# Gate products of two heads in one PSUM tile, the last sums by token tile, and a warm-up of ten products

## The chip, the cores and the metric

The kernel runs on one core of one Trainium2 chip. The time is device microseconds of one execution, from three runs: a median of 764.66 us (764.39 to 766.47). The core has five engines that work side by side: TensorE (PE, with its weight loads shown as PEld), VectorE (DVE), ScalarE (ACT), GpSimd (POOL) and SyncE (SP), which here only issues DMAs. Each engine runs its own list of instructions in order; a semaphore lets one wait for another.

## What is computed

One layer of a decoder block, for 512 tokens of 1024 channels, all float32:

```python
p = x @ W_in + b_in      # u | v | q | k | v | r | low-rank gate | branch gates g_A, g_B
y_A = gelu(u) * (W_s @ layer_norm(gelu(v)) + b_s)      # in chunks of 128 tokens
log_f = log_sigmoid(a_low @ w_gate2 + b_gate) / 16     # the gate of linear attention
y_B = norm(gla(q, k, v, log_f)) * silu(r)              # 4 heads, key width 128, value width 256
m = sigmoid(g_A) * y_A + sigmoid(g_B) * y_B
h = layer_norm(2**0.25 * x + m @ W_out)
out = layer_norm(2**0.25 * h + relu(h @ W_1)**2 @ W_2)  # hidden width 4096
```

## The kernel before

**Products.** Every float32 operand is split into a high and a low part (`split`, L91 to L93: ScalarE writes the high part, VectorE the difference), and a product of two operands takes three passes on TensorE. The weights come in chunks of 128 x 1024, read by SyncE's queue into three raw buffers (`raw`, L114), split into `wh` and `wl`, of which there are seven pairs. A raw buffer is free for the next read once both halves of the split are done.

**Stages.** The start (L240 to L267) warms TensorE with products of ones (`wu`, L241) while the first input arrives, and then makes q and k of the first two heads (`first`). The values v of the gating unit follow in two halves of four token tiles each (`row_unit`, `ps` L208). Then come eight groups of u, q and k of the last two heads, the values, the branch gates and W_out, and last the feed-forward part, three quarters of which use a seven-product scheme (`m`, L898) for two-by-two blocks of quarters, and the last quarter plain products (`f`, L984).

**Attention beside it.** A plan by slots (`plan_pair`) puts the work of linear attention between these groups: after each group of 24 matmuls on TensorE, one slot's jobs are issued. For a pair of heads that is: the gate products (`gates`, L358) and from them `lf` and its running sum `cum`; for three levels the differences `kt` on VectorE (L403) and `qt` on GpSimd (L413), their exponentials on ScalarE (L424, L425), the products with k and q on VectorE (L426, L431), and the scores on TensorE (`sc`, L472), which VectorE copies under a mask into `AT` (L484).

**Values of the gating unit.** Each token tile of v passes VectorE (`vt`, L579), ScalarE's gelu (L581), VectorE's statistics (L582) and, in the second half, an aggregate (L564), three small instructions on GpSimd (`rs_sg`, L171, L174, L566) and the normalisation on ScalarE (L567).

**Order.** TensorE's instructions stand as the code writes them. Up to the end of W_out the order on VectorE, ScalarE and GpSimd is chosen by a scheduler from the dependences and its own estimates; behind that point it is the code's. So a change in one place can move instructions of other engines a long way off. ScalarE loads a table (`ACT_TABLE_LOAD`) whenever the next function is not in the one it holds.

**PSUM.** There are eight banks of 512 columns: four for `ps_m` (main products), two for `ps_a` (one tile of 512 columns in each, tag `aux`) and two for `ps_s` (one tile of 1024 columns, tag `sc`, for scores). The two gate products of a pair go to two `aux` tiles, which they share with `pa`, `pm`, `pt`, `po` and `pb`.

**Last stage.** The quarters of the feed-forward output lie in `acc`. `together` (L905) adds up whole quarters of two token tiles (128 x 1024 elements) and folds in the residual; most of it runs between the last of the seven products and the first plain products, and inside the first token tile of these.

## Time and profile before

| | |
|---|---|
| median of three runs | 764.66 us (764.39 to 766.47) |
| the profiled execution | 764.65 us, its span 762.9 us |
| TensorE busy | 750.0 us (98%) |
| VectorE busy | 489.4 us (64%) |
| ScalarE busy | 356.3 us (47%) |
| GpSimd busy | 68.1 us (9%) |
| mean granted TensorE clock | 0.996 |

Times of the profile are counted from the first instruction of the span. The profiled execution lies 1.7 us above its span and within 0.01 us of the median, so that what moves the span can be added to either. A row of the timeline gives start, duration, engine, line, operation, what is written from what, the count, and in brackets the idle time before it and what ended that. Instructions overlap a little: a matmul of 512 columns lasts 0.39 us by its row, and the next begins 0.23 us after it.

### The profile page before, as it was taken

The page shows a single profiled execution, that of the slowest core. Times are in us where ns is not written, and L with a number is a line of the kernel's source. Part 1 is how long each engine was busy: PE and PEld are TensorE (multiplying, and loading weights), DVE is VectorE, ACT ScalarE, POOL GpSimd, SP SyncE. Part 2 cuts the span into 40 slices and gives each one's busy share as a digit, 9 for nine tenths or more (in the row PEclk, how much of TensorE's full clock was granted, in tenths as well). Part 3 has the DMA queues.
Part 4 walks back from the last instruction along what each step waited for, and adds up shares of the span by engine and source line. Part 5 has one row for each costly group of instructions (what it writes and reads, how often), then busy time and mean ns, then how long its engine had stood idle before and what let it go on. Part 6 is the DMA issues. An engine that isn't in the chain of part 4 may idle for free.

```text
span 762.9 us, 8863 instructions
## 1 busy us (share of the span) xinstructions
PE 750.0 (98%) x3504; PEld 628.3 (82%) x3504; DVE 489.4 (64%) x587; ACT 356.3 (47%) x457; POOL 68.1 (9%) x86
## 2 busy tenths in 40 slices
PE   9998999999999999999999999999999999999996
PEld 8887888878888888888888988888888888888785
DVE  7369767668766542454548535774678667778975
ACT  7376864354146444444322444554554544445300
POOL 1015400013302212000001000000000000000011
PEclk9999999999999999999999999999999999999999
DMA  8523332110341232323231423444244433434111
GB/s 338 201 97 104 104 131 82 61 53 26 111 138 56 78 129 82 113 90 104 89 125 63 153 83 99 136 148 142 73 148 139 138 109 113 164 112 165 56 56 55
DMA packets 25465, 85.15 MB, mean 112 GB/s; under 512 B 3088, under 2 KB 3344, under 8 KB 25424
## 3 DMA queue, kind: packets, MB, share of 16 engines
q1 hardware_dynamic: 25280, 84.33, 32.7%
q8 instruction: 27, 0.44, 0.2%
q10 hardware_dynamic: 144, 0.26, 0.1%
q14 instruction: 14, 0.11, 0.0%
HBM read 82.48 MB, written 2.10 MB: 111 GB/s over the span
## 4 chain that ended last, share of the span: by engine, by line
PE 88%; DVE 5%; ACT 3%; issue 2%; POOL 1%; DVEq 0%; POOLq 0%
PE f L602 23%; PE m L898 14%; PE ps L208 12%; PE gb L602 6%; PE r L602 6%; PE u L602 6%; PE f L984 5%; PE ga L602 4%; PE first L265 3%; PE qk L602 2%; PE sc L472 2%; DVE wl L93 1%; POOL qt L413 1%; PE po L498 1%; PE po L500 1%
## 5 line engine op out<-in xcount | busy, mean ns | idle before, releaser
L93 DVE TENSOR_TENSOR wl<-raw,wh 128x1024 fp32r<-128x1024 f32 x141 | 175.0, 1251 | 137.2 <-ACT wh L92 130.6
L92 ACT CAST wh<-raw 128x1024 fp32r<-128x1024 f32 x141 | 145.3, 1045 | 122.7 <-PE ps L208 27.5
L602 PE MATMUL f<-xh,wh 128*128 128x512 f32 (+1 forms) x288 | 105.4, 366 | 0.0
L602 PE MATMUL f<-xl,wh 128*128 128x512 f32 (+1 forms) x288 | 105.2, 365 | 0.0
L602 PE MATMUL f<-xh,wl 128*128 128x512 f32 (+1 forms) x288 | 105.2, 365 | 0.0
L898 PE MATMUL m<-wh,oh 128*128 128x512 f32 x168 | 65.4, 389 | 0.0
L898 PE MATMUL m<-wl,oh 128*128 128x512 f32 x168 | 65.4, 389 | 0.0
L898 PE MATMUL m<-wh,ol 128*128 128x512 f32 x168 | 65.4, 389 | 0.0
L602 PEld LDWEIGHTS f<-xh,wl 128*128 128x128 f32 x288 | 54.3, 189 | 8.8
L602 PEld LDWEIGHTS f<-xl,wh 128*128 128x128 f32 x288 | 54.3, 189 | 8.7
L602 PEld LDWEIGHTS f<-xh,wh 128*128 128x128 f32 x288 | 54.3, 189 | 8.6
L208 PE MATMUL ps<-wh,xh 128*128 128x512 f32 x128 | 51.3, 401 | 0.0
L208 PE MATMUL ps<-wl,xh 128*128 128x512 f32 x128 | 50.1, 391 | 0.0
L208 PE MATMUL ps<-wh,xl 128*128 128x512 f32 x128 | 50.1, 391 | 0.0
L827 ACT ACTIVATE F<-f 128x512 f32<-128x512 f32 (+1 forms) x28 | 15.0, 537 | 72.4 <-PE f L602 72.4
L127 DVE TENSOR_TENSOR raw<-raw,raw 128x1024 f32<-128x1024 f32 x30 | 36.7, 1222 | 8.4 <-DMA raw<-in_w_all 8.4
L413 POOL TENSOR_TENSOR qt<-cum 128x768 f32<-128x768 f32 (+2 forms) x18 | 31.4, 1774 | 115.8 <-DVE cum L368 102.9
L898 PEld LDWEIGHTS m<-wl,oh 128*128 128x128 f32 x168 | 31.6, 188 | 6.6
L898 PEld LDWEIGHTS m<-wh,ol 128*128 128x128 f32 x168 | 31.5, 188 | 6.6
L898 PEld LDWEIGHTS m<-wh,oh 128*128 128x128 f32 x168 | 31.5, 188 | 6.5
L993 POOL TENSOR_TENSOR rs_l<-rs_l,nhalf 128x1 f32<-128x1 f32 x4 | 4.0, 988 | 328.6 <-DVE rs_l L992 328.6
L92 ACT CAST oh<-d 128x1024 fp32r<-128x1024 f32 x15 | 15.8, 1050 | 36.4 <-DVE d L824 36.4
(231 smaller groups left out, 1528.5 us busy)
## 6 DMA issues: line engine op xcount, KB each, us to landing
raw<-in_w_all SPq DMA_DIRECT2D x136, 512.0 KB, 3.3
bufB<-in_head SPq DMA_DIRECT2D x4, 512.0 KB, 7.9
xr<-in_x SPq DMA_DIRECT2D x8, 256.0 KB, 3.7
out<-bufA SPq DMA_DIRECT2D x8, 256.0 KB, 2.0
bufA<-in_head SPq DMA_DIRECT2D x3, 512.0 KB, 5.3
brow<-in_b_in SPq DMA_DIRECT2D x4, 256.0 KB, 5.9
g<-in_ln_g SPq DMA_DIRECT2D x2, 512.0 KB, 4.4
b<-in_ln_b SPq DMA_DIRECT2D x2, 512.0 KB, 4.3
```

What stands on the lines that cost most here:

```text
L92: nc.scalar.copy(hi, src)
L93: nc.vector.tensor_tensor(lo, src, hi.bitcast(F32), op=ALU.subtract)
L127: nc.vector.tensor_tensor(raw, raw, other[0], op=ALU.add if STREAM[i][0] == "sum" else ALU.subtract)
L208: nc.tensor.matmul(ps, s_, m_, start=(k == 0 and i == 0), stop=(k == KT - 1 and i == 2))
L265: nc.tensor.matmul(first[e], s_, m_[:, k, :], start=(k == 0 and i == 0), stop=(k == KT - 1 and i == 2))
L413: getattr(nc, DIFF_Q).tensor_tensor(qv[:, :, s0 : s0 + n, :], c4[:, :, d:4, :], c4[:, :, 0:n, h - 1 : h].broadcast_to([P, na, n, h]), op=A ...
L472: nc.tensor.matmul(sc[:, c, 0:192], pr.kt[:, jc * P : (jc + 1) * P], pr.qt[:, jc, :], start=True, stop=True)
L498: nc.tensor.matmul(po, pr.AT[:, j, c, :], vs, start=True, stop=(c == 0))
L602: nc.tensor.matmul(ps, s_, m_, start=(k == 0 and i == 0), stop=(k == KT - 1 and i == 2))
L827: nc.scalar.activation(dst, ps, AF.Relu)
L898: nc.tensor.matmul(ps, s_, m_, start=(k == 0 and i == 0), stop=(k == 3 and i == 2))
L984: nc.tensor.matmul(ps, s_, m_, start=(f == 0 and i == 0), stop=(f == 7 and i == 2))
```

## The change

- The warm-up is ten products of 128 columns instead of seven of 128 and five of 64. Each product of ones shows as two records.
- The two gate products of a pair go into the two halves of one `ps_s` tile, tag `sc`, instead of two `aux` tiles.
- `together` works on one token tile (128 x 512) at a time. Before the last stage only the sums for token tile 0 of quarter 7 remain; the others are written into the last stage, behind the statistics of a piece.

```diff
-WARM = (128,) * 7 + (64,) * 5
+WARM = 10
-    for n in WARM:
-        nc.tensor.matmul(wu[:, :n], ones, ones[:, :n], start=True, stop=True)
+    for i in range(WARM):
+        nc.tensor.matmul(wu[:, :P], ones, ones, start=True, stop=True)
...
+        both = ps_s.tile([P, 2, T], F32, name=f"pz{hp}", tag="sc")
         for j in range(2):
             h = 2 * hp + j
-            pz = ps_a.tile([P, 512], F32, name=f"pz{h}", tag="aux")
+            pz = both[:, j, :]
             nc.tensor.matmul(pz, w2s[:, h * DK : (h + 1) * DK], a_sb, start=True, stop=True)
...
-    def together(m, terms, h=None):
-
+    def together(m, t, terms, h=None):
+
+        z = acc[m][:, t, :]
         for sign, n in terms:
-            nc.vector.tensor_tensor(acc[m], acc[m], acc[n], op=ALU.add if sign > 0 else ALU.subtract)
+            nc.vector.tensor_tensor(z, z, acc[n][:, t, :], op=ALU.add if sign > 0 else ALU.subtract)
...
         if ORDER[n] == 4:
-            together(7, ((1, 4),))
+            together(7, 0, ((1, 4),))
         if ORDER[n] == 1:
-            together(6, ((1, 3),))
-            together(7, ((1, 1),))
+            together(7, 0, ((1, 1),))
...
-    together(7, ((-1, 5),))
-    together(3, ((1, 5),), (0, 1))
+    together(7, 0, ((-1, 5),))
+    later = {
+        (0, 0): [(6, 0, ((1, 3),)), (3, 0, ((1, 5),), (0, 1))],
+        (0, 1): [(7, 1, ((1, 4), (1, 1), (-1, 5))), (6, 1, ((1, 3),)), (3, 1, ((1, 5),), (0, 1))],
+        (1, 0): [(4, t, ((1, 2),), (1, 0)) for t in range(2)],
+        (1, 1): [(6, t, ((1, 1), (-1, 2))) for t in range(2)],
+    }
...
             nc.vector.tensor_add(z[:, sl], z[:, sl], ps)
-            if t == 0:
-                together(*(((4, ((1, 2),), (1, 0))), (6, ((1, 1), (-1, 2))))[pi])
             nc.vector.bn_stats(st2[t][:, pi, :], z[:, sl])
+            for part in later.get((t, pi), ()):
+                together(*part)
```

Three places show what the change does to the order. Lines of the changed kernel lie one above those of the kernel before in the middle of the program (L358 is L359 there), and in `together` two more; numbers behind names are buffers.

The first is TensorE at the first pair's gate products, with the semaphore that an instruction waits for. Before:

```order
L208 MATMUL ps_1_419<-wl_357,xh 128x512
L208 MATMUL ps_1_419<-wh_356,xl 128x512
L358 MATMUL pz_451<-a_sb,w2s 128x512 [waits PE_49]
L358 MATMUL pz_455<-a_sb,w2s 128x512
L208 MATMUL ps_2_470<-wh_342,xh 128x512
L208 MATMUL ps_2_470<-wl_343,xh 128x512
```

Changed:

```order
L208 MATMUL ps_1_417<-wh_354,xl 128x512
L359 MATMUL pz_449<-a_sb,w2s 128x512
L359 MATMUL pz_449<-a_sb,w2s 128x512 [waits DVE_49]
L208 MATMUL ps_2_467<-wh_340,xh 128x512
L208 MATMUL ps_2_467<-wl_341,xh 128x512
```

Both products now write one tile (`pz_449`), and the second waits for VectorE: for the semaphore's value that the reading of the first half, `lf` of the first head (L361 before, L362 now), raises. That instruction in turn waits for ScalarE's `ab` of the same half. The second pair has the same wait; there both products waited for VectorE before as well, the first for the copy `KD` (L391) and the second for `mx` (L649), which hold the two `aux` tiles.

The second is ScalarE in the second half of v, around the exponential of the second level's `kt`. Before:

```order
L567 ACTIVATE bufB<-bufB,rs_sg_632 128x1024
L581 ACT_TABLE_LOAD
L581 ACTIVATE bufB<-vt_2_671 128x512
L92 CAST wh_697<-raw_522 128x1024
L424 ACT_TABLE_LOAD
L424 ACTIVATE kt_1_744<-kt_1_744 128x1024
L567 ACTIVATE bufB<-bufB,rs_sg_676 128x1024
L92 CAST wh_709<-raw_534 128x1024
L92 CAST wh_721<-raw_562 128x1024
```

Changed:

```order
L377 ACT_TABLE_LOAD
L377 ACTIVATE QI_314<-cum_447 128x1024
L568 ACTIVATE bufB<-bufB,rs_sg_629 128x1024
L582 ACT_TABLE_LOAD
L582 ACTIVATE bufB<-vt_2_668 128x512
L92 CAST wh_694<-raw_519 128x1024
L92 CAST wh_706<-raw_531 128x1024
L568 ACTIVATE bufB<-bufB,rs_sg_673 128x1024
L92 CAST wh_718<-raw_559 128x1024
L425 ACT_TABLE_LOAD
L425 ACTIVATE kt_1_741<-kt_1_741 128x1024
```

Between the gelu of the third token tile (`vt_2`) and the exponential of `kt_1` stood one cast; now three casts stand there and the normalisation of that token tile (`rs_sg_673`), for which ScalarE has to wait for VectorE's statistics and GpSimd. `QI`, which stood ahead of the second tile's gelu, has moved behind it.

The third is VectorE at the end of the seven products and the begin of the last stage. Before, from the last product of quarter 1 on:

```order
L875 TENSOR_TENSOR acc_3168<-acc_3168,m_1_1_5250 128x512
L908 TENSOR_TENSOR bufB<-bufB 128x2x512
L908 TENSOR_TENSOR bufB<-bufB,acc_3168 128x2x512
L93 TENSOR_TENSOR Fs<-Flast,Fs 128x512 x4
L93 TENSOR_TENSOR wl_5315<-raw_5228,wh_5314 128x1024
L93 TENSOR_TENSOR xl<-Flast,xh 128x512 x4
L875 TENSOR_TENSOR acc_3170<-acc_3170,m_5_0_5328 128x512
L93 TENSOR_TENSOR xl<-raw_5261,xh 128x1024
L93 TENSOR_TENSOR wl_5352<-raw_5273,wh_5351 128x1024
L93 TENSOR_TENSOR wl_5362<-raw_5318,wh_5361 128x1024
```

Changed:

```order
L876 TENSOR_TENSOR acc_3164<-acc_3164,m_1_1_5246 128x512
L910 TENSOR_TENSOR bufB<-bufB,acc_3164 128x512
L93 TENSOR_TENSOR Fs<-Flast,Fs 128x512 x4
L93 TENSOR_TENSOR wl_5310<-raw_5224,wh_5309 128x1024
L93 TENSOR_TENSOR xl<-Flast,xh 128x512 x4
L876 TENSOR_TENSOR acc_3166<-acc_3166,m_5_0_5323 128x512
L93 TENSOR_TENSOR xl<-raw_5257,xh 128x1024
L93 TENSOR_TENSOR wl_5347<-raw_5269,wh_5346 128x1024
L93 TENSOR_TENSOR wl_5357<-raw_5313,wh_5356 128x1024
```

One sum of two token tiles is gone from here and the other is half as wide; the splits of the last operands stand that much earlier.

## The prediction

> **What bounds the kernel now.** I read the page's first part, then who waited for whom on TensorE, then the timeline around each wait, and the windows for the clock.

> ```profile
> span 762.9 us, 8863 instructions
> PE 750.0 (98%) x3504; PEld 628.3 (82%) x3504; DVE 489.4 (64%) x587; ACT 356.3 (47%) x457; POOL 68.1 (9%) x86
> ...
> PE sc L472 <- DVE qt L431: 2.1, 1, 2.1
> PE sc L472 <- DVE AT L484: 0.3, 1, 0.3
> ```

> TensorE works for all but 12.9 us, so a change pays or costs only where TensorE stands still or runs slowly. The waits (total, times, longest) name few such places. The largest costs more than its 2.1 us:

> ```profile
> 64.46 0.39 PE L208 MATMUL ps<-wh,xl 128*128 128x512 f32 x1
> 66.96 2.61 PE L472 MATMUL sc<-qt,kt 128*128 128x192 f32 x8 [2.12 <-DVE qt L431]
> ...
> 75.48 1.46 PE L472 MATMUL sc<-qt,kt 128*128 128x192 f32 x8
> ...
> 82.23 0.39 PE L602 MATMUL u<-xh,wh 128*128 128x512 f32 x1
> ...
> 63.84:67.25 3.41, 1.29 (x7) 0.82 (x6) 3.41 (x4) 1.54 (x2) 2.09 (x2) 1.00 0.05 17
> 67.00:70.67 3.67, 3.67 (x12) 3.38 (x13) 2.95 (x5) 3.19 (x3) 0.51 (x2) 0.54 0.14 26
> 155.97:159.38 3.41, 2.12 (x10) 1.47 (x10) 3.35 (x6) 1.97 (x4) 0.00 (x0) 1.00 0.30 101
> ```

> From one `sc` to the next group's end there is the same work twice, 8 small matmuls and 24 large ones: 75.48 - 66.96 = 8.52 us the first time, 82.23 - 75.48 = 6.75 the second. The window rows (length, busy time of PE, PEld, DVE, ACT, POOL, then the granted clock) say why: 0.54 from 67.00 to 70.67, after a stretch in which PE was busy for 1.29 of 3.41 us. So an idle time of 66.96 - 64.69 = 2.27 us is followed by some 3.4 us at half clock, which costs 8.52 - 6.75 = 1.8 us more. The stretch around the second wait, with PE busy for 2.12 of 3.41 us, keeps 1.00.

> **The change, part by part.** *Warm-up.*

> ```profile
> 1.07 5.14 PE L241 MATMUL wu<-ones 128*128 128x128 f32 x24 [1.07 <-POOL bal L284]
> 6.02 1.17 PE L265 MATMUL first<-xh,wh 128*128 128x512 f32 x4
> ...
> L241 PEld LDWEIGHTS wu<-ones x24: 192/333/333, 1.1 to 5.9; 128*128 128x128 f32 x24
> ...
> 4.29 0.62 ACT L255 CAST xh<-bufA 128x512 fp32r<-128x512 f32 x1 [1.58 <-DMA bufA<-in_head]
> 5.53 0.68 DVE L257 TENSOR_TENSOR xl<-bufA,xh 128x512 fp32r<-128x512 f32 x1
> ```

> 24 records take 4.95 us, 0.206 each; 20 end about 0.8 earlier, near 5.25. The first operand is there at 4.91, so nothing else holds the first product. The next operand, `xl`, comes at 6.21, about when four products that begin at 5.25 are through. But weight loads last 333 ns in most of the warm-up and 192 at its end: the array speeds up only about 5.8, so that half of the 0.55 us in between is lost. Bounds -0.3 and -0.8; I take **-0.5**, nearer the middle since the late loads are few.

> *First pair's gate products.*

> ```profile
> 42.41 0.62 PE L358 MATMUL pz<-a_sb,w2s 128*128 128x512 f32 x2
> 43.56 0.75 DVE L361 TENSOR_SCALAR lf<-pz,cols_sb 128x512 f32<-128x512 f32 x1 [0.26 <-ACT ab L360]
> 43.95 0.68 ACT L360 ACTIVATE ab<-pz,cols_sb 128x512 f32<-128x512 f32 x1
> ...
> 50.55 0.68 DVE L579 TENSOR_TENSOR vt<-ps,brow 128x512 f32<-128x512 f32 x1
> 73.18 1.05 ACT L376 ACTIVATE QI<-cum 128x1024 f32<-128x1024 f32 x1
> ```

> The second product used to follow the first by 0.23 us (42.64). Now it waits until `lf` has read the first half: 43.56 + 0.75 + 0.04 = 44.35. Behind it in TensorE's list stand all further products, so TensorE loses 1.8 us there. That by itself costs nothing, since TensorE came 2.27 us too early to the scores at 66.96. What counts is the work that leads to the scores: the second `ab` begins at 44.35 + 0.39 + 0.04 = 44.78 instead of 43.95, 0.83 later.

> *The scores of the second level.* This is the term that decides. The work up to the gelu of the third token tile (82.03 below) is later by the 0.83, and since the exponential of the first `qt` now stands behind a gelu and its table loads; it is earlier by 0.60, because the sums `cum` go ahead of the `vt` at 50.55, and by 1.05, because `QI` has gone behind the second tile's gelu. I take the sum as +0.1, with -0.7 and +1.0 as bounds. Behind that gelu:

> ```profile
> 82.03 0.63 ACT L581 ACTIVATE bufB<-vt 128x512 f32<-128x512 f32 x1
> 82.56 1.04 ACT L92 CAST wh<-raw 128x1024 fp32r<-128x1024 f32 x1
> 83.62 1.28 ACT L424 ACT_TABLE_LOAD   x1
> 84.92 1.06 ACT L424 ACTIVATE kt<-kt 128x1024 f32<-128x1024 f32 x1
> 86.05 1.25 ACT L567 ACTIVATE bufB<-bufB,rs_sg 128x1024 f32<-128x1024 f32 x1
> ...
> 85.75 0.27 POOL L566 TENSOR_SCALAR rs_sg<-mv_sg,rs_sg 128x1 f32<-128x1 f32 x1
> 86.01 1.23 DVE L426 TENSOR_TENSOR kt<-kt,k 128x1024 f32<-128x1024 f32 x1 [0.88 <-ACT kt L424]
> 87.67 1.46 PE L472 MATMUL sc<-qt,kt 128*128 128x192 f32 x8
> ```

> Before, `kt` was ready at 86.01 + 1.23 = 87.24, 0.43 us ahead of TensorE. Now ScalarE comes to it over the normalisation of that tile. From the gelu's end (82.66) to the end of the last small GpSimd instruction (86.02) it is 3.36 us, and two casts fit in. So, with the gelu at 82.1: its end 82.7, `rs_sg` 86.1, normalisation to 87.3 (the next begins 1.16 behind it), cast to 88.3, table load to 89.6, exponential to 90.7, VectorE's product to 91.9, `sc` at 92.0 instead of 87.67: **+4.3**. Lower bound: if VectorE's and GpSimd's share took no longer than the two casts (1.95 by the row at 82.56), 1.4 less, and 0.7 from the gelu: +2.2. Upper: +5.3.

> TensorE's own work would bring it there sooner: `sc` of the first level at about 67.9 (its `qt` about 1 us later than before), one group at full clock to 74.65, and 87.67 - 75.48 = 12.2 more to 86.85. It stands still for 5.1 us, more than twice what halved the clock at 67, so I add that price: **+1.8**. Nothing behind it wins this back: the list of waits has none between here and the second pair's gate products.

> *Second pair's gate products.*

> ```profile
> 156.06 0.50 PE L358 MATMUL pz<-a_sb,w2s 128*128 128x512 f32 x1
> 157.85 0.51 PE L358 MATMUL pz<-a_sb,w2s 128*128 128x512 f32 x1 [1.29 <-DVE mx L649]
> 157.71 0.74 DVE L361 TENSOR_SCALAR lf<-pz,cols_sb 128x512 f32<-128x512 f32 x1
> ```

> Here the second product waited for `mx`, which held an `aux` tile. That wait goes, but `lf` of the first half stands right behind `mx` on VectorE: its end is 157.71 + 0.74 = 158.45, the product at 158.50 instead of 157.85. **+0.65**: the new wait outlasts the old one. The bounds are 0, if VectorE took `lf` first, which its list does not, and +0.75.

> *Last sums.*

> ```profile
> 744.77 0.69 DVE L985 TENSOR_TENSOR bufB<-bufB,f 128x512 f32<-128x512 f32 x1 [4.02 <-PE f L984]
> ...
> 704.42 1.22 DVE L908 TENSOR_TENSOR bufB<-bufB 128x1024 f32<-128x1024 f32 x1
> 705.55 1.22 DVE L908 TENSOR_TENSOR bufB<-bufB,acc 128x1024 f32<-128x1024 f32 x1
> 709.10 1.22 DVE L93 TENSOR_TENSOR wl<-raw,wh 128x1024 fp32r<-128x1024 f32 x1
> 714.38 2.35 DVE L93 TENSOR_TENSOR wl<-raw,wh 128x1024 fp32r<-128x1024 f32 x2
> ...
> 713.75 1.05 ACT L92 CAST wh<-raw 128x1024 fp32r<-128x1024 f32 x1 [2.58 <-DMA raw<-in_w_all]
> ...
> 713.62 0.39 PE L984 MATMUL f<-xh 128*128 128x512 f32 x1
> ...
> 717.36 0.39 PE L984 MATMUL f<-wh,Fs 128*128 128x512 f32 x1
> ```

> Nine steps of 0.227 would be 2.04 us; TensorE takes 717.36 - 713.62 = 3.74 over them, 1.7 too long, waiting for VectorE's splits. The change takes one sum out ahead of them (1.13 to the next begin) and halves the other (by 0.54): 1.67 earlier. The splits then end 0.1 to 1.8 us ahead of their use. The last chunk must also be read earlier; its raw buffer is freed by the split at 709.10, which moves as well. If the read did not move, 0.1 would be all; if it moves by as much, 1.7. I take **-1.6**, since buffer and split hang together. From there on VectorE has 18 sums of one token tile (0.60 each to the next begin) instead of 7 of two (1.14), 2.8 us more. They are spread over the first three token tiles, where VectorE idles 4.02 us by the row at 744.77 and the four banks of `ps_m` keep TensorE going; without that cover they would cost up to the 2.8.

> **The sum**, on the profiled 764.65: -0.5 + 4.3 + 1.8 + 0.65 - 1.6 = +4.65, so **769.3 us**. With the bounds of each term: 766.8 to 772.0.

> **Rivals.** *The scores are not late* (not slower). If `kt` of the second level came by 86.8, 5 us sooner than I reckon, TensorE would not stop at that place. The first scores would begin 0.9 later than now but save the halved clock: 0.9 - 1.8 - 0.5 + 0.65 - 1.6 = -2.35, so 762.3. For it: TensorE then loses its largest wait. Against it: ScalarE's list is fixed, and the normalisation cannot start before GpSimd has ended.

> *The late scores, but a short wait.* If TensorE stood for under some 2 us and the clock stayed whole: -0.5 + 2.0 + 0.65 - 1.6 = +0.55, so 765.2. That needs 2.3 off the term, the edge of its bounds.

> *Half clock after the second gate, too.* TensorE would stand there from 156.29 to 158.50, 2.2 us; 2.27 halved the clock at 67, 1.56 at 157 did not. Whether it does hangs on how the wait lies in the clock's stretches of 3.41 us, which I cannot place to better than 1 us. It adds 1.8, less the 0.3 that a later `sc` waits for `AT` anyway: 770.8. [...]

> **Chances.** Forecast 0.63 (its own range 767 to 771), second halving 0.20, short wait 0.07, not late 0.10. A measurement of this kernel tells from no change what differs by over 0.3%, 2.3 us, so between 762.4 and 767.0 counts as the same. The third case and a small part of the forecast fall there, and the last splits about evenly: faster 0.06, the same 0.15, slower 0.79. Range 765.6 to 771.9: it leaves out the case on the other side and the far ends.

> **What would show it.** In the changed profile, `sc` of the second level waits 4 to 5 us for VectorE's `kt`, and the window behind it shows a granted clock near 0.5, while that at 67 to 71 need not. The first gate's second product begins 1.9 us after the first, the second pair's 2.4. The first product begins near 5.25, and the last stage's first group takes about 5.5 us instead of 7.1. If the second level's scores wait for nothing, the forecast is wrong; if they wait but the clock stays at 1.00, it is 1.8 too high.

## The result: slower by 1.1%, and by more than forecast

| | before | changed |
|---|---|---|
| median of five runs | 764.66 us (764.03 to 766.47) | 773.32 us (773.12 to 774.12) |
| ratio | | 1.0113, interval 1.0098 to 1.0127 |
| the profiled execution, and its span | 764.65 us, 762.9 us | 774.12 us, 772.4 us |
| mean granted TensorE clock | 0.996 | 0.989 |

The direction was forecast. The size was not: 769.3 was said, with a range to 771.9. Beside the experiments below the kernel before takes either near 764.3 or near 766.4 us, at a granted clock of 0.996 to 0.998 in the first case and of 0.997 or 0.998 in the second, so that more half clock does not explain the slower times, and what does is open.

The engines' busy times in the changed kernel and its list of TensorE's waits (total, times, longest):

```profile
PE 753.0 (97%) x3500; PEld 630.8 (82%) x3500; DVE 491.7 (64%) x597; ACT 362.4 (47%) x461; POOL 67.4 (9%) x86
...
PE pz L359 <- DVE lf L362: 3.7, 2, 2.1
PE sc L473 <- DVE qt L432: 3.6, 1, 3.6
PE sc L473 <- DVE kt L427: 3.4, 1, 3.4
```

Of the waits before (2.1 us for `qt`, 1.3 for `mx`), the first has grown to 3.6, the second has gone, and two have come: for `lf`, in each of the two pairs, and 3.4 for `kt`. TensorE's timeline of the changed kernel shows where these lie:

```profile
5.16 1.17 PE L265 MATMUL first<-xh,wh 128*128 128x512 f32 x4
...
41.89 0.39 PE L359 MATMUL pz<-a_sb,w2s 128*128 128x512 f32 x1
43.84 0.50 PE L359 MATMUL pz<-a_sb,w2s 128*128 128x512 f32 x1 [1.57 <-DVE lf L362]
...
69.74 2.90 PE L473 MATMUL sc<-qt,kt 128*128 128x192 f32 x8 [3.60 <-DVE qt L432]
...
93.87 2.90 PE L473 MATMUL sc<-qt,kt 128*128 128x192 f32 x8 [3.43 <-DVE kt L427]
...
103.68 0.59 PE L635 MATMUL pb<-wst,ones 128*128 128x512 f32 x1
...
165.17 0.48 PE L359 MATMUL pz<-a_sb,w2s 128*128 128x512 f32 x1
167.75 0.50 PE L359 MATMUL pz<-a_sb,w2s 128*128 128x512 f32 x1 [2.11 <-DVE lf L362]
...
721.35 0.39 PE L990 MATMUL f<-wh,Fs 128*128 128x512 f32 x1
...
726.82 0.40 PE L990 MATMUL f<-wh,Fs 128*128 128x512 f32 x1
```

Each begin is set against that of the same instruction before. The first `sc` was at 66.96 (now 2.78 later) and the second level's at 87.67 (6.20 later). The first `pb` was at 94.43:

```profile
94.43 1.88 PE L634 MATMUL pb<-wst,ones 128*128 128x512 f32 x4
```

It is 9.25 later. The last stage began at 710.22 and is 11.13 later, and the span ends 9.5 later. Between 6.20 and 9.25 lies half clock, which the stretches of 3.41 us around the three long waits show (length, busy time of PE, PEld, DVE, ACT, POOL, granted clock):

```profile
65.94:69.35 3.41, 0.20 (x1) 0.00 (x0) 2.24 (x4) 3.38 (x4) 0.00 (x0) 1.00 0.32 126
69.35:72.76 3.41, 3.02 (x9) 3.05 (x10) 2.77 (x6) 3.37 (x4) 0.55 (x2) 0.50 0.31 95
89.83:93.24 3.41, 0.61 (x3) 0.18 (x1) 1.97 (x2) 3.37 (x4) 0.00 (x0) 1.00 0.24 72
93.24:96.65 3.41, 2.78 (x9) 2.81 (x10) 2.61 (x4) 2.68 (x4) 1.19 (x1) 0.50 0.43 161
96.65:100.07 3.42, 3.42 (x10) 2.65 (x9) 1.48 (x4) 2.34 (x3) 0.84 (x3) 0.50 0.44 153
164.92:168.33 3.41, 1.30 (x9) 0.90 (x8) 3.38 (x5) 1.33 (x4) 0.00 (x0) 1.00 0.28 94
168.33:171.74 3.41, 3.41 (x10) 2.63 (x9) 0.75 (x1) 3.36 (x4) 0.00 (x0) 0.50 0.17 65
```

After each stretch in which PE was busy for 0.20, 0.61 and 1.30 us, the clock is 0.50. It is so for one stretch at 69 and at 168, but for two at 93.

Why did `kt` come so late? The other engines of the changed kernel ahead of the scores at 93.87:

```profile
81.48 0.63 ACT L582 ACTIVATE bufB<-vt 128x512 f32<-128x512 f32 x1
82.02 1.99 ACT L92 CAST wh<-raw 128x1024 fp32r<-128x1024 f32 x2
87.91 1.25 ACT L568 ACTIVATE bufB<-bufB,rs_sg 128x1024 f32<-128x1024 f32 x1 [3.91 <-POOL rs_sg L567]
91.41 1.06 ACT L425 ACTIVATE kt<-kt 128x1024 f32<-128x1024 f32 x1
...
79.70 6.00 POOL L414 TENSOR_TENSOR qt<-cum 128x768 f32<-128x768 f32 x3 [0.82 <-PE sc L473]
85.78 1.08 POOL L171 TENSOR_SCALAR rs_sg<-mv_sg 128x1 f32<-128x1 f32 x1
87.61 0.26 POOL L567 TENSOR_SCALAR rs_sg<-mv_sg,rs_sg 128x1 f32<-128x1 f32 x1
...
80.62 2.02 DVE L404 TENSOR_TENSOR kt<-cum 128x1024 f32<-128x1024 f32 x1
83.81 2.98 DVE L93 TENSOR_TENSOR wl<-raw,wh 128x1024 fp32r<-128x1024 f32 x2
```

In the kernel before, the same instructions of GpSimd and VectorE read:

```profile
79.40 3.53 POOL L413 TENSOR_TENSOR qt<-cum 128x768 f32<-128x768 f32 x3
83.92 1.08 POOL L171 TENSOR_SCALAR rs_sg<-mv_sg 128x1 f32<-128x1 f32 x1 [0.99 <-DVE mv_sg L564]
...
78.09 1.21 DVE L403 TENSOR_TENSOR kt<-cum 128x1024 f32<-128x1024 f32 x1
82.69 0.69 DVE L582 BATCH_NORM_STATS2 sgst<-bufB 128x6 f32<-128x512 f32 x1 [3.39 <-ACT bufB L581]
```

ScalarE's order is as forecast, and so is the gelu (81.48). But GpSimd's last small instruction ends 87.87, 5.76 us behind the gelu's end (82.11); before it was 3.36. GpSimd's three differences take 6.00 us instead of 3.53. Before, VectorE was idle while they ran, and GpSimd then waited 0.99 us for VectorE's mean (`mv_sg`). Now VectorE's `kt` difference, copies and splits stand beside them, the `kt` difference, too, takes 2.02 instead of 1.21, and the small instructions begin only when the differences are through. The rows suggest that the two engines slow each other; an experiment below takes the differences away.

### The profile page after: what moved, and what is told of

The parts are those of the page before. It is cut to its first block, busy times and chain, and to the rows that moved or that the text cites. A ratio compares the mean times of both kernels' runs of the same rounds, so it can differ in the third digit from the quotient of the medians.

```text
span 772.4 us, 8871 instructions
## 1 busy us (share of the span) xinstructions
PE 753.0 (97%) x3500; PEld 630.8 (82%) x3500; DVE 491.7 (64%) x597; ACT 362.4 (47%) x461; POOL 67.4 (9%) x86
## 4 chain that ended last, share of the span: by engine, by line
PE 89%; DVE 5%; ACT 3%; issue 2%; DMA 1%; POOL 0%; DVEq 0%; ACTq 0%
PE f L603 23%; PE m L899 15%; PE ps L208 13%; PE f L990 6%; PE gb L603 6%; PE r L603 6%; PE u L603 5%; PE ga L603 4%; PE qk L603 3%; PE first L265 3%; PE sc L473 2%; DVE wl L93 1%; PE po L499 1%; PE pm L648 1%; PE po L501 1%
## 5 line engine op out<-in xcount | busy, mean ns | idle before, releaser
L93 DVE TENSOR_TENSOR wl<-raw,wh 128x1024 fp32r<-128x1024 f32 x141 | 176.0, 1258 | 144.8 <-ACT wh L92 138.2
L92 ACT CAST wh<-raw 128x1024 fp32r<-128x1024 f32 x141 | 145.7, 1045 | 125.6 <-PE ps L208 29.1
L208 PE MATMUL ps<-wh,xh 128*128 128x512 f32 x128 | 51.2, 400 | 0.0
L208 PE MATMUL ps<-wh,xl 128*128 128x512 f32 x128 | 49.9, 389 | 0.0
L208 PE MATMUL ps<-wl,xh 128*128 128x512 f32 x128 | 49.8, 389 | 0.0
L92 ACT CAST oh<-d 128x1024 fp32r<-128x1024 f32 x15 | 15.8, 1050 | 36.4 <-DVE d L825 36.4
```

Of the source, the lines that this page charges most:

```text
L92: nc.scalar.copy(hi, src)
L93: nc.vector.tensor_tensor(lo, src, hi.bitcast(F32), op=ALU.subtract)
L208: nc.tensor.matmul(ps, s_, m_, start=(k == 0 and i == 0), stop=(k == KT - 1 and i == 2))
```

## The experiments

Twelve kernels were run, four at a time on one chip, each time beside the kernel before, whose median was 764.21, 764.42 and 764.39 us there. The diffs of fillers are shortened to what they issue. Where kernels of different chips are compared, it is by what they take over the kernel before on their own chip; the change takes 8.7 us over it.

### The three edits apart

The gate products alone (the tile `both` put into the kernel before), the gates taken back out of the change, and each of the other two edits alone:

```diff
# gates_alone, on the kernel before
+        both = ps_s.tile([P, 2, T], F32, name=f"pz{hp}", tag="sc")
-            pz = ps_a.tile([P, 512], F32, name=f"pz{h}", tag="aux")
+            pz = both[:, j, :]
# without_gates, on the changed kernel: the same, the other way round
# warm_alone, on the kernel before
-WARM = (128,) * 7 + (64,) * 5
+WARM = (128,) * 10
# sums_alone, on the kernel before: together() with a token tile t, and later, as in the change
```

> The kernel before with the gate products alone moved into one scores tile; warm-up and last sums stay as before. If the gate products are the whole loss (theory), the sums by token tile still gain 1.6 us and the warm-up 0.5, so this kernel must be slower than the changed one by 2.1: 775.4 us, with the first scores of the second level some 6 to 7 us later than at 87.67 us. Rival, that the sums by token tile or the warm-up also cost something elsewhere: 773 or less.

> The changed kernel with the gate products back in two aux tiles; shorter warm-up and sums by token tile stay. Theory: 764.66 - 0.5 - 1.6 = 762.5 us, the last stage's first group without a wait, the first scores still waiting about 2 us for qt. Rival, that the two edits cost elsewhere: 764 us or more.

> The kernel before with the last sums alone by token tile, as in the change. Theory (the last stage's first group ends 1.6 earlier, and the later sums hide under TensorE): all of the stages as before, the last stage 1.6 shorter, 762.6 to 763.3. Rival (the sums in the last stage take VectorE's cover and give it back): 764.3 to 764.9.

> The kernel before with the warm-up of ten 128-column products alone. Theory (the first product begins 0.7 to 0.9 earlier, and 0.1 to 0.5 of it lasts to the end): 764.1 to 764.6. Rival (a written order that comes out otherwise, as one vt and one exponential change places here, costs or brings more than 1 us): outside 763.5 to 765.5.

| kernel | median | ratio to before |
|---|---|---|
| gates alone | 774.13 us | 1.0134 (1.0118 to 1.0149) |
| sums alone | 762.83 us | 0.9960 (0.9945 to 0.9975) |
| warm-up alone | 764.45 us | 0.9988 (0.9977 to 0.9999) |
| change without gates | 762.39 us | 0.9978 (0.9968 to 0.9988) |

The gates carry the whole loss. Alone they take 9.9 us over the kernel before, 1.3 more than the change, where 2.1 more were expected. In their own run the second level's scores wait 3.5 us for `kt` and the clock is halved at the same three places (means of 0.83 from 64 to 74, 0.72 from 90 to 102 and 0.91 from 155 to 173, as in the change). Without them, the changed kernel is faster than the one before; its list of waits is that of before, without the waits for splits in the last stage:

```profile
PE sc L472 <- DVE qt L431: 2.0, 1, 2.0
PE pz L358 <- DVE mx L649: 1.3, 1, 1.3
```

The sums bring 1.6 us. The warm-up alone brings nothing that lasts: its first product begins 0.66 us earlier (5.36 for 6.02), but the first gate product at 42.49, where it began at 42.41 before, and the last stage 0.01 earlier. Nor is an early start a sign of it: in the run of the gates alone, with the old warm-up, the first product begins at 5.26 and the first gate product at 41.66, earlier than the change's 41.89. So two kernels with the old warm-up lie 0.75 us apart at the first gate product, more than the 0.5 that the edit was to bring.

### The wait of the products, or the order of the lists

If the product's wait for `lf` itself were the cost, issuing both products ahead of their readers would cure it. If the place of the `kt` exponential on ScalarE is the cost, it would not, and what moves the exponential back would.

```diff
# both_first, on the changed kernel: both products, then the readers
+            nc.tensor.matmul(both[:, j, :], w2s[:, h * DK : (h + 1) * DK], a_sb, start=True, stop=True)
+        for j in range(2):
+            h = 2 * hp + j
-            nc.tensor.matmul(pz, w2s[:, h * DK : (h + 1) * DK], a_sb, start=True, stop=True)
# five_fill and seven_fill, on the changed kernel, ahead of the first scores (n = 5 or 7)
+        for i in range(n):
+            nc.tensor.matmul(fl, ones_r, xh[:, 0, :], start=True, stop=True)
```

The fillers write an `aux` bank that nobody reads. They matter here less for TensorE than because five of them make the scheduler write ScalarE's list with the `kt` exponential ahead of the normalisation, as before the change, while seven leave it behind.

> The changed kernel with both gate products issued ahead of the four instructions that read them, so that no product waits for a reader, in the same tile. ScalarE's list still has kt's exponential of the second level behind the third tile's normalisation. Order theory (what costs is where that exponential stands): the second level's scores still come 4 to 6 us late, the second pair's gate costs nothing: 769 to 772 us. Wait theory (what costs is the product that waits for the readers): 762 to 764 us.

> The changed kernel with five extra products of ones (1.1 us of work) on TensorE ahead of the first scores, where it waited 3.6 us. The second gate product still waits for the reader of the first, but the scheduler puts kt's exponential of the second level ahead of the third tile's normalisation again, as in the kernel before. Order theory: the second level's scores wait for nothing or under 1 us, no half clock behind them: 766 to 769 us. Wait theory: 773 us as the changed kernel.

> As the run with five fillers ahead of the first scores, but with seven. Two products more are 0.45 us of TensorE's idle time and cost nothing by themselves; they tip the written order, so that the second level's exponential of kt stands behind the third tile's normalisation again, as in the changed kernel. Theory (the order on ScalarE is what costs): the first scores behave as with five (clock whole at 67 to 71, +2.4 to +3.5), then the second level's scores wait for kt again by 3 us or more, with half clock behind it, and the time is 770 to 774, 4 to 6 us above the 766.9 of five fillers. Rival (five fillers won because they kept the clock up at the first scores): the time is that of five fillers, 766.3 to 767.5.

| kernel | median | ratio to before | second level's scores, against before |
|---|---|---|---|
| both products first | 769.00 us | 1.0063 (1.0046 to 1.0080) | +4.61 us |
| five fillers | 766.88 us | 1.0035 (1.0022 to 1.0049) | +1.75 us |
| seven fillers | 771.55 us | 1.0086 (1.0070 to 1.0102) | +6.36 us |

With both products first there is no wait for `lf` at all, and yet the first pair's scores wait for `kt` (twice now, at the first level's, begun at 68.18, as well as at the second level's, begun at 92.28):

```profile
PE sc L475 <- DVE kt L429: 6.8, 2, 3.5
```

The five and the seven fillers differ in ScalarE's order. First five, then seven:

```profile
84.98 1.06 ACT L425 ACTIVATE kt<-kt 128x1024 f32<-128x1024 f32 x1
88.54 1.24 ACT L574 ACTIVATE bufB<-bufB,rs_sg 128x1024 f32<-128x1024 f32 x1 [2.49 <-POOL rs_sg L573]
...
89.42 1.46 PE L479 MATMUL sc<-qt,kt 128*128 128x192 f32 x8
```

```profile
88.08 1.24 ACT L574 ACTIVATE bufB<-bufB,rs_sg 128x1024 f32<-128x1024 f32 x1 [3.82 <-POOL rs_sg L573]
91.57 1.06 ACT L425 ACTIVATE kt<-kt 128x1024 f32<-128x1024 f32 x1
```

With five, ScalarE still waits for `rs_sg`, but nobody waits for ScalarE: the scores at 89.42 have no idle time before them. Five take 2.7 us over the kernel before, seven 7.1, so two fillers more cost 4.5. What the gates cost besides that order is at most 4.5 us, by which five fillers stand above the change without gates on the same chip (766.88 and 762.39). And since the late exponential is there in `both_first` as well, where no product waits for `lf`, it is not that wait that brings the order. (The profiled execution with five fillers also escaped the half clock at the first scores, which the one with seven, against the expectation, did not: 1.00 and 0.84 from 64 to 74; more of this below. TensorE came to the next scores 1.1 us earlier, at 77.22 instead of 78.36, so up to that much of the 4.6 us by which the two differ at the second level's scores is the clock.)

### The half clock by itself

Fourteen fillers in the wait for `kt`, which leave ScalarE's order as it is in the change, and eight between the second pair's gate products, in the kernel with five fillers.

```diff
# filled_second_wait, on the changed kernel, ahead of the second level's first scores
+        for i in range(14):
+            nc.tensor.matmul(fl, ones_r, xh[:, 0, :], start=True, stop=True)
# five_fill_second_gate, on five_fill, ahead of the second pair's second product
+            if hp and j == 0:
+                for i in range(8):
+                    nc.tensor.matmul(fg, ones_r, xh[:, 0, :], start=True, stop=True)
```

> The changed kernel with 14 products into an unused bank ahead of the second level's first scores (14 x 0.227 = 3.2 us of work that nobody reads, in the wait of 3.43 us); the exponential of kt stays behind the third tile's normalisation. Theory (the wait moves the scores by its length, and the two stretches of half clock behind it, 93.24 for 6.83 us, come from TensorE standing still): the scores still begin at 93.7 to 94.3, the clock stays whole there, the first pb comes about 3 us earlier than in the changed kernel (+6 instead of +9.25 against the kernel before), and the time is 769.8 to 771. Rival (what follows the late scores is slow for its own reason, operands or banks that come late): pb stays at +9 and the time at 773.

> The kernel with five fillers ahead of the first scores (766.88), and eight products into an unused bank between the two gate products of the second pair (8 x 0.227 = 1.8 us, in the wait of 2.10 us there); the lists of the other engines stay the same. Theory (the second gate costs 0.8 by its wait and 1.6 by the stretch of half clock behind it, 160.54 for 3.41 us): the clock stays whole, the stage behind comes at +2.4 against the kernel before instead of +4.0, and the time is 765.3 to 766.0, unless the slack of 0.6 that the second pair's scores have takes part of it. Rival (the halving there is taken back by later waits): 766.7 to 767.1.

With the wait filled, the scores begin at 94.27 and not sooner, but the clock behind stays whole, and `pb` is 6.68 later than before instead of 9.25. The time is 770.88 us, 1.0077 (1.0061 to 1.0093): 6.5 over the kernel before where the change takes 8.7. Rows of TensorE and the stretch behind:

```profile
90.78 3.43 PE L475 MATMUL fill<-xh,ones_r 128*128 128x512 f32 x14
94.27 1.54 PE L479 MATMUL sc<-qt,kt 128*128 128x192 f32 x8
...
94.19:97.60 3.41, 3.36 (x18) 3.03 (x18) 2.13 (x3) 2.14 (x3) 1.66 (x2) 1.00 0.28 108
```

From these scores to `pb` the kernel lost 3.05 us in the change (6.20 to 9.25) and 0.08 with the wait filled by work that nobody reads (6.60 to 6.68). So the two stretches of half clock cost 3.0 us at this place. The whole time fell by only 2.2, although in this profile the clock stayed whole behind the second pair's gate too (1.00 from 155 to 173, with 1.78 us busy in the stretch around its wait).

Between the second pair's products the eight fillers kept the clock whole too (1.00 from 155 to 173, 0.91 with five fillers): the way from the second product to the next stage, which took 1.6 us longer than before in the run with five, takes no longer than before here. Its time, though, is 766.43 us, 1.0013 (1.0001 to 1.0025), or 2.0 over the kernel before, against 2.7 with five alone: 0.6 instead of the 0.9 to 1.6 expected. A reason is in the same profile: now the first scores are halved, which they were not in the profile with five, though program and wait are alike up to there. The rows with five fillers, then with those of the second gate added:

```profile
70.36 1.54 PE L479 MATMUL sc<-qt,kt 128*128 128x192 f32 x8 [2.44 <-DVE qt L432]
...
68.38:71.79 3.41, 1.43 (x9) 1.46 (x10) 3.41 (x5) 3.36 (x4) 0.00 (x0) 1.00 0.00 0
71.79:75.21 3.42, 3.42 (x17) 2.79 (x16) 2.55 (x7) 3.34 (x3) 1.07 (x3) 1.00 0.42 153
```

```profile
69.77 2.33 PE L483 MATMUL sc<-qt,kt 128*128 128x192 f32 x8 [2.46 <-DVE qt L436]
...
66.94:70.35 3.41, 0.95 (x6) 0.61 (x5) 2.63 (x4) 3.38 (x4) 0.00 (x0) 1.00 0.01 5
70.35:73.77 3.42, 3.42 (x11) 3.04 (x11) 2.69 (x6) 3.32 (x4) 1.06 (x3) 0.50 0.46 153
```

Two waits of nearly the same length, 2.44 and 2.46 us: one is cut in two by the border of a stretch and followed by 1.00, the other lies within one and is followed by 0.50. (The border at 68.38 is counted back from the half clock that began at 160.54 there, 27 times 3.413 us.) So of two waits of this length one was followed by half clock and the other was not, and the mean clock of one kernel differs between its executions too: 0.989 to 0.994 in the five of the change.

### What made the third tile's normalisation so late

If GpSimd and VectorE slow each other, taking GpSimd's three differences away from beside VectorE's work must bring the scores earlier. They go to VectorE, where they stand behind all that leads to the normalisation; ScalarE's and TensorE's lists stay as they are in the change.

```diff
# diffs_on_vector, on the changed kernel
+            eng = "vector" if (hp, lv) == (0, 2) else DIFF_Q
-            getattr(nc, DIFF_Q).tensor_tensor(
+            getattr(nc, eng).tensor_tensor(
```

> The changed kernel, with one thing altered: the three qt differences of the first pair's third level run on VectorE instead of GpSimd (they come there behind the vt of 86.70, so nothing moves ahead of the normalisation's inputs, and the lists of ScalarE and TensorE are the same to the last row). In the changed kernel these three took GpSimd 6.00 us from 79.70 (3.53 in the kernel before), and the small instructions for the third tile's normalisation stood behind them until 85.78. Theory (contention: GpSimd and VectorE slow each other with their two-input operations, and GpSimd's end sets the second level's scores): without them the small instructions begin as soon as VectorE's mean is there, near 83, VectorE's kt difference takes 1.2 instead of 2.0, the normalisation starts near 85.2 instead of 87.9, and the second level's scores come at 91.0 to 91.6 instead of 93.87, with a wait of about 1 us instead of 3.4 and no half clock behind it. The third mix of that stage (first pb) is then 5 to 6 us earlier and the whole time 767 to 769, with the second pair's gate as it was. Rival (the late gelu and the table loads alone make the scores late, GpSimd's share is covered by the casts): the scores stay at 93.5 to 94, and the time at 773.

It took 771.06 us, 1.0078 (1.0060 to 1.0096): 6.6 over the kernel before, so 2.0 better than the change, where 4 to 6 were expected. The engines' rows:

```profile
80.66 1.21 DVE L404 TENSOR_TENSOR kt<-cum 128x1024 f32<-128x1024 f32 x1
83.09 2.36 DVE L93 TENSOR_TENSOR wl<-raw,wh 128x1024 fp32r<-128x1024 f32 x2
...
83.23 1.17 POOL L171 TENSOR_SCALAR rs_sg<-mv_sg 128x1 f32<-128x1 f32 x1 [4.34 <-DVE mv_sg L566]
84.48 1.40 POOL L174 TENSOR_TENSOR rs_sg<-rs_sg,nhalf 128x1 f32<-128x1 f32 x1
85.98 1.07 POOL L568 TENSOR_SCALAR rs_sg<-mv_sg,rs_sg 128x1 f32<-128x1 f32 x1
...
93.04 1.76 PE L474 MATMUL sc<-qt,kt 128*128 128x192 f32 x8 [2.44 <-DVE kt L428]
```

VectorE's `kt` difference is back at 1.21 us and GpSimd begins at 83.23, as said. But then its three small instructions, of one column each, take 1.17, 1.40 and 1.07 us, while VectorE runs two splits, a sum and a difference. In the changed kernel the last of them took 0.26 us (its row at 87.61), when VectorE had nothing to do. So the contention is shown, and it also ate most of what its removal would bring: `rs_sg` ends 0.82 earlier, not 2.7. The clock behind was halved for one stretch instead of two (a mean of 0.86 from 90 to 102, where the change has 0.72). Moving the small instructions to VectorE as well was not tried, so how much the scores would gain with no contention at all is not shown.

### A version without the wait at the first scores

The best kernel of the study, the change without the gates, still stands 1.97 us ahead of the first scores and is halved behind them (0.50 from 67.93 to 71.34). Nine fillers, and then three, were put there.

```diff
# without_gates_fill (n = 9) and without_gates_fill3 (n = 3), on without_gates, ahead of the first scores
+        for i in range(n):
+            nc.tensor.matmul(fl, ones_r, xh[:, 0, :], start=True, stop=True)
```

> The changed kernel with the gate products back in two aux tiles (762.39 by its run), and nine products into an unused bank in the 1.97 us that TensorE stands ahead of the first scores (9 x 0.227 = 2.04 us). Theory (that wait halves the clock for one stretch of 3.41 us, which costs 1.5 to 1.8): no half clock at 67.9, everything from there to the end of the stage 1.5 to 1.8 earlier, the time 760.6 to 761.2, against the kernel before 0.9955. Rival (a later wait takes it back, as the second pair's scores or the shift of the stretches): 762.2 to 762.6.

> The changed kernel with the gate products back in two aux tiles, and three products into an unused bank ahead of the first scores, where nine made VectorE's mask copies come behind other work and cost 4.3 us. With three, two of the three copies stand one instruction later than without fillers. Theory (the wait halves the clock when TensorE is busy for little more than half a stretch; three products raise it from 42% to 62% of 3.41 us if the wait lies in one stretch): no half clock at 67.9, the copies still in time, 760.8 to 761.8. Rival (the copies come too late again, or the clock halves anyway): 762.4 or more.

Both were slower than the change without gates, at 766.72 us (1.0027, 1.0016 to 1.0037) and 766.86 us (1.0019, 1.0008 to 1.0029) where that had 0.9978. The clock at the first scores was whole in both (1.00 from 64 to 74, where that had 0.83). But VectorE's mask copies of the first scores had moved behind other work, and the next scores stood for them, with half clock behind that wait (means of 0.79 with nine and 0.89 with three from 74 to 90). From the list of waits of the kernel with nine (that with three has the same line):

```profile
PE sc L478 <- DVE AT L490: 4.1, 2, 3.8
```

So the rival held here: the order that the fillers brought cost more than the clock that they saved. The half of a stretch that the expectation for three fillers names was the author's estimate, and no run shows it as the limit: 1.44 us busy (42%) in the change without gates was followed by half clock, but 1.48 with seven fillers (43%) and 1.78 with the second wait filled (52%) were not. The fastest kernel stays the change without the gates.

## Why the prediction was right and where it was wrong

**Warm-up** (-0.5): the number was met in this profile, by luck. The first product came at 5.16 (5.25 said) and the first pair's gate 0.52 earlier, but alone the warm-up leaves nothing by that gate, and a kernel without it was there earlier still. That the edit is worth 0.5 is not shown.

**First pair's gate** (no cost by itself): the wait was right, the second product came 1.95 us after the first (1.9 said), and TensorE still stood idle for 3.60 us ahead of the first scores.

**The scores of the second level** (+4.3): the mechanism was right, the size was not. Against a program earlier by 0.52 they are 6.72 late. The step that failed: "From the gelu's end (82.66) to the end of the last small GpSimd instruction (86.02) it is 3.36 us", carried over to the changed kernel. It was 5.76. The gelu came at 81.48 for 82.1, which is the earlier program and no more, and what lies behind GpSimd took 6.00 us for 5.9. The 3.36 came from a profile in which GpSimd's three differences had run beside an idle VectorE and were through before the mean was there; the change itself moved VectorE's work beside them. They ended at 85.70, so that GpSimd's first small instruction began 1.9 us after the mean was there (83.89; before it was 0.1), and VectorE's statistics began 0.8 after the gelu's end, where it had been 0.03. Not even the upper bound of the term, 5.3, held it.

**The half clock behind it** (+1.8): 3.05. That TensorE would stand there long enough was right, though it stood 3.43 us and not 5.1: the first scores came at 69.74 rather than 67.9 and were halved as well, so that TensorE itself arrived late. (The first scores were late because ScalarE stood 3.69 us for a `vt` that VectorE wrote behind three splits; these took 2.1 to 2.3 us each beside GpSimd's differences, where one takes 1.2 alone.) The failed step is "so I add that price": the price was of one stretch, and there were two. The stretch from 93.24, in which work began again only at 93.87, held 2.78 us of it and half clock followed; the one from 69.35 held 3.02 and full clock followed.

**Second pair's gate** (+0.65): the wait itself was exact: the next product is 0.65 further behind than the one ahead. But the rival "half clock after the second gate, too", held at 0.20, came on top: +1.62, of which 0.7 was given back before the scores at 202 and 0.3 lost again. In sum +1.88. The row at 164.92 shows the stretch ahead: 1.30 us busy in 3.41, and half clock after it.

**Last sums** (-1.6): right, -1.65, and -1.6 in the run with the sums alone. The last stage's first group took 5.47 us (5.5 said), and the later sums hid under TensorE.

The sum by the span: -0.52 + 6.72 + 3.05 + 1.88 - 1.65 = +9.48, where +4.65 was said. Of the 4.8 missing, 2.4 lies in the step to GpSimd's end, which I put down to its contention with VectorE by the rows, 1.25 is the second stretch of half clock, 1.2 the second gate's. The prediction's range for this sum was also added up too narrowly: its own bounds give 766.2 to 772.1, not 766.8 to 772.0, and 773.32 lies outside either.

This sum holds for the profiled execution, the longest of the five. The other four took 773.1 to 773.4 us at a clock of 0.991 to 0.994 instead of 0.989. Those at 0.994 had some two stretches of half clock less, by an estimate from these figures (one stretch of 3.41 us lowers the mean by 0.002), and were only 0.8 to 0.9 us shorter. What the half clock is worth over the whole kernel is therefore less certain than its price at one place.

## What to carry to other kernels

Moving two products of 0.4 us into another tile can be free on TensorE where they stand and still cost 10 us, if it tips the order in which another engine's list is written: compare the lists of all engines, find the instruction that has moved behind something that waits, and follow that chain. A duration on GpSimd or VectorE may be carried over from a profile only if what runs on the other of the two at that time stays the same: here 3.53 us became 6.00. And price a wait on TensorE by its clock as well: in the changed kernel 2.11 us of idle time within one stretch of 3.41 us (164.92 to 168.33) brought one stretch at half clock, and at 93.24 a restart 0.63 us into the halved stretch was followed by a second.
